# A hybrid decoder step: split MLP weights kept in DRAM, four MLP token groups, the RWKV solve on GpSimd, a planner with other latencies

## The chip, the cores and the metric

The kernel runs on 1 core of one Trainium2 chip. The time is the device time of one launch in microseconds (us), the median of the runs. Five engines work in parallel, each on its own in-order stream of instructions: PE (TensorE, matmuls), DVE (VectorE), ACT (ScalarE), POOL (GpSimd) and SP (SyncE, which here does nothing but issue DMAs). An instruction that waits for a semaphore holds back all that stands behind it on its engine.

## The reference

One decoder layer for 2048 prompt tokens and 64 sample tokens (8 sequences of 8), width 1024, all in f32:

```python
h = rms_norm(x, norm1_g) * (1.0 + sc1) + sh1
proj = h @ w_in                                   # 1024 -> 3328: q, k, v and the RWKV row P
att = combine_dilations(branches)                 # three dilated windows, 8 heads of 64
r, decay, kr, vr, kk, a, g = rwkv7_inputs(P, P_prev, ...)
o, S = wkv7_scan(wkv0, r, decay, kr, vr, kk, a)   # S = S*w + (S.-kk)(kk*a)' + v k', per token
mix = concat([att, rwkv7_output(o, ...)]) @ w_out
x = x + gt1 * mix
h2 = rms_norm(x, norm2_g) * (1.0 + sc2) + sh2
x = x + gt2 * (square(relu(h2 @ w_ff1)) @ w_ff2)  # 1024 -> 4096 -> 1024
y = rms_norm(x, normf_g)
```

The sample tokens attend to a cache of past keys and values and carry an RWKV state each.

## The kernel before

**Numbers.** Every large product is computed from f32 operands that are each split in two: `hi`, the value rounded to the matmul's fast f32 type, and `lo`, the rest. `mm3` makes three matmuls for each 128-row slice: hi by hi, hi by lo, lo by hi (L319, L320, L321). A weight block of 128x1024 numbers is therefore loaded (tile `stg`, 512 KB), copied to `hi` by ACT and subtracted to `lo`, five eighths of it by POOL and three eighths by DVE (`split`, L257 and L261). Tiles `whi`, `wlo` are blocks of w_in; `wh`, `wl` are blocks of w_out, w_ff1 and w_ff2 (`wload`).

**Stages.** The prompt goes in four windows of 512 tokens. `i0` to `i3` are the input projections, `a0` to `a3` the attention of a window (four head pairs each), `r0` to `r3` its RWKV part, `s` the sample tokens. RWKV works in groups of 128 tokens, four per window, 16 in all (and one for the sample). For each group `rw_elem` makes decays and vectors, `rw_mats` makes triangular matrices with PE (PSUM tile `aps`, result `AT`), `rw_solve` inverts them: two DMAs `dA<-AT` and `sol<-dA` spread 32 small 32x32 matrices over 128 partitions, 31 steps of two elementwise operations each run on `sol` (L707, L713, on DVE), DMAs `dT<-sol` and eight `AT<-dT` bring the result back, and PE finishes with two sets of small matmuls (`zps`, L725 and L729). `rw_chunk` then advances the state twice (`px`, `pu`, `psS`). The tile `sol` exists once; `AT`, `bkT` and `F1` exist once, so that the matrices of a group are made when the group before has been through `rw_chunk`.

**MLP.** Five token groups: three of 512, then 256 + 64 sample tokens, then 256. For group w, `m` loads the concatenated heads (`mixd`, in DRAM), `p` does w_out, residual and norm in halves of at most 320 tokens, `f` runs eight rounds of w_ff1 (four blocks) and w_ff2 (four blocks). Each group loads and splits every weight block again; w_out is loaded once per half. Group 3 needs the RWKV result of the first half of the last window, group 4 that of the second half. Group 4 has its own buffers, in memory that the vector stages have given up.

**Order.** A planner of the framework places the instructions of all engines by its own model of their durations, and by priorities that come from the string `ORDER`: `f2:8@2190-2740` says that eight rounds of group 2 belong to 2190 to 2740 of the plan's time. What the planner decides is the fixed order on each engine. MLP and input matmuls (PSUM tile `mmps`) are what PE does while the vector stages run.

Of the kernel before, what the change touches and what calls it, by code (L numbers as in the profile page):

```python
# [18 lines left out]
D = 1024  # L19
KD = 8  # L20
# [20 lines left out]
m3@2730-2731 f2:99@2740-2741 p3@2741-2790 f3:2@2790-2990 m4@2840-2841 p4@2841-2890 f3:99@2840-3040  # L41
f4:99@3000-3200
# [79 lines left out]
class Step:  # L122
    def __init__(self, tc, I, O):
        self.tc, self.nc, self.I, self.O = tc, tc.nc, I, O
        self.es = ExitStack()
        self.bg = None
        self.lo_eng, self.nw, self.nwb = [tc.nc.gpsimd], 0, 0
# [14 lines left out]
    def setup(self):  # L142
# [18 lines left out]
        self.mixd = self.dr.tile([D, SEQ + NS], F32, name="mixd")  # L161

# [92 lines left out]
    def split(self, hi, lo, src, eng=None):  # L255
# [17 lines left out]
    def norm_B(self, xt, pool, rows, A, B, hhi, hlo, c0, sample, psp, pstag):  # L273
        nc = self.nc
        h32 = pool.tile([128, KD, 128], F32, name="h32", tag="h32")
        for hb in range(2):
# [29 lines left out]
            eng = nc.vector if hb else nc.gpsimd  # L306
            eng.tensor_tensor(lo, h32[:, sl, 0:rows], hi.bitcast(F32), op=ALU.subtract)  # L307
# [23 lines left out]
    def w_in(self, c0, G):  # L331
        nc = self.nc
# [4 lines left out]
        for h in range(2):  # L337
            sl = slice(128 * h, 128 * h + 128)
            sg = G.tile([128, KD, 128], F32, name="stg", tag="stg")
            src = self.I["w_in"][0][:, c0 + 128 * h:c0 + 128 * h + 128]  # L340
            nc.sync.dma_start(sg, src.rearrange("(k p) c -> p k c", p=128))
            self.split(hi[:, :, sl], lo[:, :, sl], sg)
# [116 lines left out]
    def rwkv_setup(self):  # L459
# [8 lines left out]
        self.masks_s = cst("masks_s", [128, 128])  # L468
# [161 lines left out]
    def rw_mats(self, V, psv, r, nch, masks):  # L630
# [8 lines left out]
        AO = V.tile([64, nch * 8, 64], F32, name="AO", tag="AO")  # L639
# [7 lines left out]
        for c in range(nch):  # L647
# [6 lines left out]
            for par in (1, 0):  # L654
# [10 lines left out]
        r.update(F1=F1, bkT=bkT, AT=AT, AO=AO)  # L665
# [3 lines left out]
    def rw_bonus(self, V, psv, r):  # L669
# [12 lines left out]
    def rw_solve(self, V, psv, r, nch):  # L682
# [6 lines left out]
        for b in range(2):  # L689
            o = 32 * b  # L690
            nc.sync.dma_start(dA[:, b].rearrange("u s t -> s u t"), AT[o:o + 32, :, o:o + 32])
# [12 lines left out]
        for s in range(31):  # L704
            m, n = 31 - s, s // 4 + 1
            t3 = tmp[:, 0:m * n].rearrange("p (j i) -> p j i", i=m)
            nc.vector.tensor_tensor(  # L707
# [5 lines left out]
            nc.vector.tensor_tensor(T[:, 0:n, s + 1:32], T[:, 0:n, s + 1:32], t3, op=ALU.add)  # L713
# [5 lines left out]
        nc.vector.transpose(TZ[0:32, 0], AT[64:96, :, 0:32])  # L719
# [4 lines left out]
        for u in range(nu):  # L724
            nc.tensor.matmul(pz[96:128, u], AT[0:32, u, 32:64], TZ[0:32, 0, u], start=True, stop=True, tile_position=(0, 96))  # L725
# [6 lines left out]
    def rw_chunk(self, V, psv, r, c, nxt, po):  # L732
# [23 lines left out]
        nc.gpsimd.tensor_tensor(s0, UV[0:64, c], dcb, op=ALU.mult)  # L756
# [73 lines left out]
    def rwkv_window(self, w, V, psv):  # L830
# [8 lines left out]
        for g in range(g0, g0 + 4):  # L839
# [5 lines left out]
            for par in range(2):  # L845
                for c in range(2):
                    for o in (0, 64) if par else (0,):
                        nc.gpsimd.tensor_copy(
# [41 lines left out]
    def att_window(self, w, hp, V, psv):  # L890
# [10 lines left out]
        if w > 0:  # L901
            nc.gpsimd.dma_start(kT[:, :, :, 0:w], self.kTd[hp][:, :, :, 0:w])
# [145 lines left out]
    def rwkv_sample(self, V, psv):  # L1048
# [36 lines left out]
        self.rw_mats(V, psv, r, 1, self.masks_s)  # L1085
# [195 lines left out]
    def wload(self, src, n, G):  # L1281

        nc = self.nc
        nk = 1024 // n
        sg = G.tile([128, nk, n], F32, name="stg", tag="stg")
        nc.sync.dma_start(sg, src.rearrange("(k p) c -> p k c", p=128))
        hi = G.tile([128, nk, n], F32R, name="wh", tag="wh")
        lo = G.tile([128, nk, n], F32R, name="wl", tag="wl")
        self.nw += 1
        self.split(hi, lo, sg, self.lo_eng[self.nw % len(self.lo_eng)])  # L1290
# [343 lines left out]
```

## Time and profile before

| | |
|---|---|
| Time, median of 3 runs | 3894.37 us (3886.09 to 3895.49) |
| The profiled execution | 3875.28 us, its span 3873.5 us |
| PE busy | 3376.6 us (87%) |
| DVE, ACT, POOL busy | 2425.2 (63%), 1690.4 (44%), 1052.3 us (27%) |
| DMA | 505.27 MB, 43.3% of the 16 engines' time on SP's queue |
| Granted PE clock | 0.935 of full speed, mean |

Full speed of PE is 2.4 GHz; the lower of its two levels is 1.2 GHz, and a mean of 0.94 in a stretch says how long it was at either. PE idle is the length of a stretch less PE busy. A matmul's own duration in a row is longer than the distance to the next one, since matmuls overlap; the pace is read from a stretch without idle time. In the rows by windows the five busy times are, in this order, those of PE, PEld (weight loads), DVE, ACT and POOL, with the count of instructions behind each.

### The profile page before, as it was taken

The page shows a single profiled execution, that of the slowest core. Times are in us where ns is not written, and L with a number is a line of the kernel's source. Part 1 is how long each engine was busy: PE and PEld are TensorE (multiplying, and loading weights), DVE is VectorE, ACT ScalarE, POOL GpSimd, SP SyncE. Part 2 cuts the span into 40 slices and gives each one's busy share as a digit, 9 for nine tenths or more (in the row PEclk, how much of TensorE's full clock was granted, in tenths as well). Part 3 has the DMA queues.
Part 4 walks back from the last instruction along what each step waited for, and adds up shares of the span by engine and source line. Part 5 has one row for each costly group of instructions (what it writes and reads, how often), then busy time and mean ns, then how long its engine had stood idle before and what let it go on. Part 6 is the DMA issues. An engine that isn't in the chain of part 4 may idle for free. (4 is left out here: it accounts for less than half of the span.)

```text
span 3873.5 us, 64002 instructions
## 1 busy us (share of the span) xinstructions
PE 3376.6 (87%) x24050; PEld 2838.8 (73%) x24050; DVE 2425.2 (63%) x6052; ACT 1690.4 (44%) x3088; POOL 1052.3 (27%) x792
## 2 busy tenths in 40 slices
PE   7998898887978888898889898888889898869998
PEld 5875787777767666777767676676667776769998
DVE  3653665654656577877656765454777777645666
ACT  4542443453344355545434532344545344434354
POOL 2322231221133211223321121132112222234464
PEclk9999999888889999999999999999999999879999
DMA  7346644344243342325435244886432234354464
GB/s 245 112 138 184 169 124 129 109 84 93 78 116 119 100 129 76 100 85 168 124 98 142 75 91 118 244 256 202 124 104 85 86 88 135 110 148 142 144 188 153
DMA packets 698128, 505.27 MB, mean 130 GB/s; under 512 B 90330, under 2 KB 646540, under 8 KB 697820
## 3 DMA queue, kind: packets, MB, share of 16 engines
q1 hardware_dynamic: 685196, 488.54, 43.3%
q0 software_dynamic: 12624, 12.65, 1.3%
q8 instruction: 190, 3.11, 0.3%
q14 instruction: 118, 0.97, 0.1%
HBM read 430.77 MB, written 65.99 MB: 128 GB/s over the span
## 5 line engine op out<-in xcount | busy, mean ns | idle before, releaser
L261 POOL TENSOR_TENSOR wl<-stg,wh 128x640 fp32r<-128x640 f32 (+1 forms) x384 | 670.5, 1747 | 1655.9 <-ACT wh L257 1392.6
L257 ACT ACTIVATE wh<-stg 128x1024 fp32r<-128x1024 f32 x384 | 406.0, 1058 | 730.0 <-PE mmps L320 444.5
L319 PE MATMUL mmps<-h2hi,wh 128*128 128x256 f32 (+2 forms) x1864 | 635.8, 342 | 34.6 <-ACT wh L257 16.6
L321 PE MATMUL mmps<-h2hi,wl 128*128 128x256 f32 (+2 forms) x1864 | 635.8, 341 | 8.1 <-POOL wl L261 7.5
L320 PE MATMUL mmps<-h2lo,wh 128*128 128x256 f32 (+2 forms) x1864 | 632.7, 340 | 4.4 <-POOL h2lo L307 4.4
L320 PE MATMUL mmps<-hid,wh 128*128 128x512 f32 (+2 forms) x1280 | 469.9, 367 | 10.9 <-DVE hid L1388 10.8
L261 DVE TENSOR_TENSOR wl<-stg,wh 128x384 fp32r<-128x384 f32 (+1 forms) x384 | 304.2, 793 | 273.9 <-ACT wh L257 263.5
L319 PE MATMUL mmps<-hid,wh 128*128 128x512 f32 (+2 forms) x1280 | 469.9, 368 | 3.9 <-ACT acc L1274 2.8
L321 PE MATMUL mmps<-hid,wl 128*128 128x512 f32 (+2 forms) x1280 | 468.9, 367 | 1.1 <-POOL wl L261 0.9
L319 PEld LDWEIGHTS mmps<-h2hi,wh 128*128 128x128 f32 x1864 | 366.0, 197 | 68.7 <-ACT wh L257 18.0
L321 PEld LDWEIGHTS mmps<-h2hi,wl 128*128 128x128 f32 x1864 | 366.2, 196 | 40.0 <-POOL wl L261 9.4
L320 PEld LDWEIGHTS mmps<-h2lo,wh 128*128 128x128 f32 x1864 | 365.8, 196 | 34.5 <-POOL h2lo L307 5.1
L261 POOL TENSOR_TENSOR wlo<-stg,whi 128x640 fp32r<-128x640 f32 x104 | 183.8, 1781 | 588.2 <-ACT whi L257 523.0
L320 PEld LDWEIGHTS mmps<-hid,wh 128*128 128x128 f32 x1280 | 249.0, 195 | 45.0 <-DVE hid L1388 14.0
L319 PEld LDWEIGHTS mmps<-hid,wh 128*128 128x128 f32 x1280 | 248.3, 194 | 36.6 <-ACT acc L1274 3.4
L321 PEld LDWEIGHTS mmps<-hid,wl 128*128 128x128 f32 x1280 | 248.9, 194 | 32.0 <-issue 1.3
L1266 DVE SCALAR_TENSOR_TENSOR acc<-mmps,ada,acc 128x512 f32<-128x512 f32 (+1 forms) x280 | 179.0, 641 | 142.1 <-PE mmps L321 140.2
L319 PE MATMUL mmps<-whi,hhi 128*128 128x256 f32 (+1 forms) x816 | 242.8, 298 | 5.7 <-ACT qev L427 5.7
L320 PE MATMUL mmps<-wlo,hhi 128*128 128x256 f32 (+1 forms) x816 | 243.4, 298 | 1.2 <-POOL wlo L261 1.2
L319 PE MATMUL mmps<-hhi,whi 128*128 128x512 f32 (+2 forms) x608 | 223.5, 369 | 23.5 <-ACT pev L397 18.1
L321 PE MATMUL mmps<-whi,hlo 128*128 128x256 f32 (+1 forms) x816 | 242.7, 297 | 0.0
L320 PE MATMUL mmps<-hlo,whi 128*128 128x512 f32 (+2 forms) x608 | 222.3, 366 | 5.3 <-POOL hlo L307 5.3
(340 smaller groups left out, 6705.5 us busy)
## 6 DMA issues: line engine op xcount, KB each, us to landing
stg<-in_w_ff_dram SPq DMA_DIRECT2D x320, 512.0 KB
stg<-in_w_in_dram SPq DMA_DIRECT2D x104, 512.0 KB
stg<-in_w_out_dram SPq DMA_DIRECT2D x64, 512.0 KB
kst<-in_cache_k_dram SPq DMA_DIRECT2D x80, 256.0 KB
vst<-in_cache_v_dram SPq DMA_DIRECT2D x80, 256.0 KB
xt<-in_x_prompt_dram SPq DMA_DIRECT2D x32, 512.0 KB
wada<-in_w_ada_dram SPq DMA_DIRECT2D x32, 512.0 KB
Pd<-pev SPq DMA_DIRECT2D x56, 256.0 KB
```

What stands on the lines that cost most here:

```text
L257: nc.scalar.activation(hi, src, AF.Copy)
L261: eng.tensor_tensor(lo[:, k], src[:, k], hi[:, k].bitcast(F32), op=ALU.subtract)
L319: nc.tensor.matmul(out, wh(k), xh(k), start=k == 0, stop=False)
L320: nc.tensor.matmul(out, wh(k), xl(k), start=False, stop=False)
L321: nc.tensor.matmul(out, wl(k), xh(k), start=False, stop=k == nk - 1)
L1266: nc.vector.scalar_tensor_tensor(o, pt[:, 0:np_], gt[:, ob, 0:1], o, op0=ALU.mult, op1=ALU.add)
```

## The change

1. `wload` and `w_in` go through a new `weights`. After a given use of a block (the first for w_out and w_ff1, the second for w_ff2, the ninth for w_in, which has four) its `hi` and `lo` are written to DRAM; later uses load both, 512 KB each, with four DMAs, and split nothing. `stg`, `wh` and `wl` share seven buffers (three, three and two before).
2. Groups 3 and 4 become one of 512 + 64 tokens, in columns of 288. It takes its activations in the memory of the vector stages and its other buffers from the earlier groups.
3. The 31 steps of `rw_solve` run on POOL. `AT`, `bkT`, `F1` have two buffers, `AO` moves into `AT`; other small operations go from POOL to DVE; 32 loads of w_ada go to POOL's queue, 12 loads of `kT` to SP's.
4. `PlanCosts` changes the planner's model: 105 cycles more for each access, 2300 ns for a DMA's start, 0.443 ns for a PE cycle.

```diff
-m3@2730-2731 f2:99@2740-2741 p3@2741-2790 f3:2@2790-2990 m4@2840-2841 p4@2841-2890 f3:99@2840-3040
-f4:99@3000-3200
+m3@2730-2731 f2:99@2740-2741 p3@2741-2790 f3:99@2790-3200
...
+        self.done, self.uses, self.keep_at = set(), {}, {"in": 9, "out": 1, "ff1": 1, "ff2": 2}
...
-        self.nc.sync.dma_start(w, src.rearrange("(k p) c -> p k c", p=128))
+        (self.nc.sync if nk > 1 else self.nc.gpsimd).dma_start(w, src.rearrange("(k p) c -> p k c", p=128))
...
+    def weights(self, name, i, src, hi, lo, G, tag):
+
+        nc = self.nc
+        wd = self.wd[name][i]
+        if (name, i) in self.done:
+            for j, t in enumerate((hi, lo)):
+                for p in (slice(0, 64), slice(64, 128)):
+                    nc.sync.dma_start(t[p].bitcast(F32).rearrange("p k c -> p (k c)"), wd[p, j])
+            return
+        nk, n = lo.shape[1:3]
+        m = 1024 // nk
+        for c in range(0, n, m):
+            sg = G.tile([128, nk, m], F32, name="stg", tag=tag)
+            nc.sync.dma_start(sg, src[:, c:c + m].rearrange("(k p) c -> p k c", p=128))
+            self.split(hi[:, :, c:c + m], lo[:, :, c:c + m], sg)
+        self.uses[name, i] = n = self.uses.get((name, i), 0) + 1
+        if n == self.keep_at[name]:
+            for j, t in enumerate((hi, lo)):
+                nc.sync.dma_start(wd[:, j], t.bitcast(F32).rearrange("p k c -> p (k c)"))
+            self.done.add((name, i))
...
-                nc.vector.tensor_tensor(AT[0:64, u:u + 4], pt[0:64, :, 0:64], mb(0, 0, 64), op=ALU.mult)
-                nc.vector.tensor_tensor(AO[:, u:u + 4], pt[0:64, :, 64:128], mb(0, 64, 64), op=ALU.mult)
+                nc.vector.tensor_tensor(AT[64:128, u:u + 4], pt[0:64, :, 0:64], mb(0, 0, 64), op=ALU.mult)
+                nc.vector.tensor_tensor(AT[0:64, u:u + 4], pt[0:64, :, 64:128], mb(0, 64, 64), op=ALU.mult)
...
-            nc.vector.tensor_tensor(
+            nc.gpsimd.tensor_tensor(
                 t3,
                 A[:, s:s + 1, s + 1:32].to_broadcast([128, n, m]),
                 T[:, 0:n, s:s + 1].to_broadcast([128, n, m]),
                 op=ALU.mult,
             )
-            nc.vector.tensor_tensor(T[:, 0:n, s + 1:32], T[:, 0:n, s + 1:32], t3, op=ALU.add)
+            nc.gpsimd.tensor_tensor(T[:, 0:n, s + 1:32], T[:, 0:n, s + 1:32], t3, op=ALU.add)
...
-        raw=2, rawl=1, e2=8, F=2, bk=1, F1=1, bkT=1, AT=1, AO=1, UV=2, xx=2, Dt=1, lm=2, sgl=2, bv=1, xs=1,
+        raw=2, rawl=1, e2=7, F=2, bk=1, F1=2, bkT=2, AT=2, UV=2, xx=2, Dt=1, lm=2, sgl=2, bv=1, xs=1,
...
-    gs = [pt(512 * w, 4) for w in range(3)] + [pt(1536, 2) + [(SEQ, NS, True)], pt(1792, 2)]
-    MG = dict(h2h=1, h2l=1, acc=1, wh=3, wl=3, stg=2, hid=NHID, st=4, rlu=2)
+    gs = [pt(512 * w, 4) for w in range(3)] + [pt(1536, 4) + [(SEQ, NS, True)]]
+    MG = dict(h2h=1, h2l=1, acc=1, w=7, hid=NHID, st=4, rlu=2)
...
-                X = Tags(gm.enter_context(right("last")), {**MG, "hid": 5, "stg": 3, "wh": 4, "wl": 4, "rlu": 2})
...
+                X = Tags(gm.enter_context(right("last")), dict(h2h=1, h2l=1, acc=1))
+                B = S.mlp_tiles(TS + NS, X)
+                G = Mix(G, h2h=X, h2l=X, acc=X)
...
+    ACCESS, DMA, CYCLE = 105, 2300.0, 0.443
...
+        for k in T.ACCESS_CYCLES:
+            T.ACCESS_CYCLES[k] += self.ACCESS
+        T.DMA_START_FIXED_NS, T.PE_CYCLE = self.DMA, self.CYCLE
...
-    with tile.TileContext(nc) as tc:
+    with PlanCosts(), tile.TileContext(nc) as tc:
```

The planner's order changes everywhere. Three places are shown: the order of one engine before and after.

PE, before, where the last group of the last window waits for its solve: `aps` are its matrices, `zps` uses the solved ones, `mmps` of 320 columns are MLP matmuls of group 3.

```order
L321 MATMUL mmps<-h2hi,wl 128x320
L319 MATMUL mmps<-h2hi,wh 128x320
L320 MATMUL mmps<-h2lo,wh 128x320
L658 MATMUL aps<-F,bk 128x128 x8
...
L321 MATMUL mmps<-hid,wl 128x320
L319 MATMUL mmps<-hid,wh 128x320
L320 MATMUL mmps<-hid,wh 128x320
L725 MATMUL zps<-sol,AT 32x32 x16
```

PE, after, at the same place, up to where the MLP of the last token group begins:

```order
L674 MATMUL aps<-F,bk 128x128 x3
L785 MATMUL psS<-UV,bkT 64x64 x8
L839 MATMUL gps<-sgl,r_g_1770 128x128 x4
...
L741 MATMUL zps<-sol,AT 32x32 x16
L745 MATMUL zps<-AT,sol 32x32 x16
...
L885 MATMUL stps<-ident,state 128x64 x4
...
L343 MATMUL mmps<-h2hi,wh 128x256
```

Between the last `aps` and the first `zps` stood 302 MLP matmuls of 320 columns; now there is none, only RWKV matmuls of the group before. The same holds for the third group of the window (253 MLP matmuls before, none now).

POOL, before, in a stretch of the vector stages of the second half: parts of weight splits (`wl`), the clearing of `sol`, and small RWKV operations.

```order
L261 TENSOR_TENSOR wl<-stg,wh 128x640 x3
L701 MEMSET sol 128x256
L703 MEMSET sol 32x8 x4
L261 TENSOR_TENSOR wl<-stg,wh 128x640
L261 TENSOR_TENSOR wl<-stg,wh 128x512 x2
L848 COPY DC<-Dt 64x4 x6
L756 TENSOR_TENSOR xs<-UV,DC 64x512
```

POOL, after, at the end of one solve and the start of the next, in the third window:

```order
L723 TENSOR_TENSOR sol<-sol 128x28
L729 TENSOR_TENSOR sol<-sol 128x7x4
L265 TENSOR_TENSOR wl<-stg,wh 128x512
L723 TENSOR_TENSOR sol<-sol 128x24
...
L265 TENSOR_TENSOR wl<-stg,wh 128x640
L717 MEMSET sol 128x256
L719 MEMSET sol 32x8 x4
L265 TENSOR_TENSOR wl<-stg,wh 128x640 x2
```

The 62 steps of a solve now stand on POOL as one block with at most four other instructions inside; weight splits of the first two token groups stand before and behind it.

SP, before, at the last solve of the last window: weight loads (`stg`) between the solve's DMAs.

```order
L691 DMA dA<-AT 32x16x32 x2
L1286 DMA stg<-in_w_ff_dram 128x4x256
L502 DMA raw<-Pd 128x4x129
L698 DMA sol<-dA 128x1x1024
L1286 DMA stg<-in_w_ff_dram 128x4x256 x3
```

SP, after, at the first solve of the same window: each block now comes as two halves of `wh` and two of `wl`.

```order
L707 DMA dA<-AT 32x16x32 x2
L519 DMA raw<-Pd 128x4x129 x2
L714 DMA sol<-dA 128x1x1024
L274 DMA wl<-wd_ff_122 64x1024 x2
L274 DMA wh<-wd_ff_151 64x1024 x2
L730 DMA dT<-sol 128x256
```

Where one DMA carried a block, four do, and they stand between the steps of the solve.

## Rows read from the trace of the kernel before

**Rows 1.** The page: its head, and the busy time of each engine.

```profile
span 3873.5 us, 64002 instructions
...
PE 3376.6 (87%) x24050; PEld 2838.8 (73%) x24050; DVE 2425.2 (63%) x6052; ACT 1690.4 (44%) x3088; POOL 1052.3 (27%) x792
```

**Rows 2.** Windows A to D: length, five engines' busy, PEclk, DMA share, GB/s.

```profile
0.00:138.00 138.00, 109.85 (x600) 84.20 (x601) 50.98 (x123) 65.66 (x117) 37.56 (x37) 0.95 0.64 211
138.00:2978.00 2840.00, 2474.84 (x17807) 2039.12 (x17805) 1804.16 (x4769) 1246.38 (x2345) 664.33 (x527) 0.94 0.45 126
2978.00:3440.00 462.00, 397.51 (x2708) 328.60 (x2708) 317.47 (x727) 191.67 (x346) 129.40 (x109) 0.91 0.36 105
3440.00:3873.50 433.50, 394.39 (x2938) 386.88 (x2937) 252.61 (x436) 186.67 (x280) 220.97 (x120) 0.96 0.52 160
```

**Rows 3.** Windows: 512-column MLP, 256-column MLP, sample attention, MLP alone.

```profile
1930.00:1960.00 30.00, 30.00 (x134) 24.86 (x133) 17.68 (x57) 11.49 (x15) 8.35 (x5) 1.00 0.28 73
3720.00:3790.00 70.00, 70.00 (x584) 69.88 (x583) 46.31 (x73) 34.18 (x49) 45.12 (x25) 1.00 0.60 182
...
2400.00:2700.00 300.00, 259.50 (x2309) 209.24 (x2308) 138.19 (x258) 115.66 (x196) 66.20 (x39) 0.95 0.77 231
...
3500.00:3700.00 200.00, 192.25 (x1340) 189.03 (x1341) 125.72 (x237) 86.02 (x131) 95.08 (x53) 1.00 0.47 145
```

**Rows 4.** Waits of PE: who waited for whom, total us, times, longest.

```profile
PE ptps L1019 <- ACT s L993: 40.1, 17, 3.3
PE zps L725 <- DVE sol L719: 37.3, 8, 7.8
...
PE s2ps L958 <- DVE kT L922: 26.0, 16, 3.5
PE trps L1436 <- DVE xt L1439: 19.2, 12, 6.4
PE btps L645 <- DVE bk L620: 18.5, 5, 7.0
PE mmps L319 <- ACT pev L397: 18.1, 7, 4.9
PE mmps L319 <- ACT wh L257: 16.6, 3, 12.2
...
PE trps L1436 <- ACT acc L1268: 15.1, 14, 2.6
```

**Rows 5.** Groups of instructions: busy us, mean ns of one, idle before them.

```profile
L261 DVE TENSOR_TENSOR wl<-stg,wh 128x384 fp32r<-128x384 f32 (+1 forms) x384 | 304.2, 793 | 273.9 <-ACT wh L257 263.5 <-PE mmps L321 4.7 <-ACT st L1423 1.7
...
L713 DVE TENSOR_TENSOR sol<-sol 128x60 f32<-128x60 f32 (+24 forms) x527 | 144.6, 274 | 11.2
```

**Rows 6.** POOL: copies `DC` (min/median/max ns), and one subtraction in two sizes.

```profile
L848 POOL COPY DC<-Dt x96: 181/347/4742, 136.5 to 3218.8; 64x4 f32<-64x4 f32 x96
...
L526 POOL TENSOR_TENSOR bnl<-mr,bnh 128x512 fp32r<-128x512 f32 x16 | 21.3, 1332 | 83.1 <-ACT bnh L525 83.1
...
L526 POOL TENSOR_TENSOR bnl<-mr,bnh 128x256 fp32r<-128x256 f32 x1 | 0.7, 724 | 3.7 <-ACT bnh L525 3.7
```

**Rows 7.** Timeline, one group of r3, then the last's end: start, us, instruction.

```profile
2988.45 1.71 PE L658 MATMUL aps<-F,bk 64*128 64x128 f32 x16
...
3005.42 0.19 DVE L707 TENSOR_TENSOR sol<-sol 128x31 f32<-128x31 f32 x1 [4.95 <-DMA sol<-dA]
...
3040.85 0.34 SPq L714 DMA_DIRECT2D dT<-sol  x1
...
3051.41 1.19 PE L725 MATMUL zps<-sol,AT 32*32 32x32 f32 x32
...
3421.09 1.17 PE L729 MATMUL zps<-AT,sol 32*32 32x32 f32 x32 [0.30 <-issue]
...
3457.73 0.58 PE L319 MATMUL mmps<-h2hi,wh 128*128 128x256 f32 x1 [12.20 <-ACT wh L257]
```

**Rows 8.** Waits of SP's queue: the longest in total.

```profile
SPq L1286 <- DVE wl L261: 1249.0, 346, 14.7
```

More of the change, by code (lines that the diff above doesn't have):

```diff
@@ L161, in setup @@
         self.mixd = self.dr.tile([D, SEQ + NS], F32, name="mixd")
+        self.wd = {
+            name: [self.dr.tile([128, 2, m], F32, name=f"wd_{name}{i}") for i in range(n)]
+            for name, n, m in (("in", 13, 2048), ("out", 8, 1024), ("ff1", 32, 1024), ("ff2", 32, 1024))
+        }
+        self.done, self.uses, self.keep_at = set(), {}, {"in": 9, "out": 1, "ff1": 1, "ff2": 2}
     def params(self, G, psp):
@@ L253, in mod, with split @@
         return A, self.ada[:, 8 * sh:8 * sh + 8]
-    def split(self, hi, lo, src, eng=None):
+    def split(self, hi, lo, src):
         nc = self.nc
@@ L336, in w_in @@
         hi = G.tile([128, KD, 256], F32R, name="whi", tag=tag)
[L337 to L342, printed above, removed]
+        self.weights("in", c0 // 256, self.I["w_in"][0][:, c0:c0 + 256], hi, lo, G, "stg")
         return hi, lo
@@ L724, in rw_solve @@
         for u in range(nu):
-            nc.tensor.matmul(pz[96:128, u], AT[0:32, u, 32:64], TZ[0:32, 0, u], start=True, stop=True, tile_position=(0, 96))
+            nc.tensor.matmul(pz[96:128, u], AT[64:96, u, 32:64], TZ[64:96, 0, u], start=True, stop=True, tile_position=(64, 96))
         nc.scalar.activation(TZ[96:128, 0], pz[96:128], AF.Copy)
@@ L1084, in rwkv_sample @@
         r = self.rw_elem(V, psv, -1)
-        self.rw_mats(V, psv, r, 1, self.masks_s)
+        masks = V.tile([128, 128], F32, name="masks_s", tag="masks_s")
+        nc.sync.dma_start(masks, I["masks_s"])
+        self.rw_mats(V, psv, r, 1, masks)
         self.rw_solve(V, psv, r, 1)
@@ L1279, in gate_s, with wload @@
             self.nc.vector.tensor_tensor(a[:, k], a[:, k], gt[:, k, 1:9, None].to_broadcast([128, 8, 8]), op=ALU.mult)
-    def wload(self, src, n, G):
-        nc = self.nc
+    def wload(self, name, i, src, n, G):
         nk = 1024 // n
[L1285 to L1290, printed above, removed]
+        hi = G.tile([128, nk, n], F32R, name="wh", tag="w")
+        lo = G.tile([128, nk, n], F32R, name="wl", tag="w")
+        self.weights(name, i, src, hi, lo, G, "w")
         return hi, lo
@@ L1314, in mlp_mix @@
             for k in range(0, KD, nk):
-                sg = G.tile([128, nk, n], F32, name="stg", tag="stg")
+                sg = G.tile([128, nk, n], F32, name="stg", tag="w")
                 nc.sync.dma_start(
@@ L1333, in mlp_prep @@
             for ob in range(KD):
-                hi, lo = self.wload(I["w_out"][0][:, 128 * ob:128 * ob + 128], 128, G)
+                hi, lo = self.wload("out", ob, I["w_out"][0][:, 128 * ob:128 * ob + 128], 128, G)
                 pt = psg.tile([128, 512], F32, name="mmps", tag="mm")
@@ L1371, in ff1 @@
             for fb in fbs:
-                hi, lo = self.wload(I["w_ff1"][0][:, 128 * fb:128 * fb + 128], 128, G)
-                hd = G.tile([128, 2, T], F32R, name="hid", tag="hid")
+                hi, lo = self.wload("ff1", fb, I["w_ff1"][0][:, 128 * fb:128 * fb + 128], 128, G)
+                hd = G.tile([128, 2, TS + NS], F32R, name="hid", tag="hid")
                 W.append((hi, lo, hd))
@@ L1413, in mlp_ff @@
         c = 0
-        gf = G.tile([128, D], F32, name="gf", tag="wl")
+        gf = G.tile([128, D], F32, name="gf", tag="w")
         nc.sync.dma_start(gf, I["normf_g"].rearrange("(o d) -> o d", o=1).to_broadcast([128, D]))
@@ L1573, in tile_hybrid_step, with __enter__, __exit__ @@
     S.es.close()
+class PlanCosts:
+    ACCESS, DMA, CYCLE = 105, 2300.0, 0.443
+    def __enter__(self):
+        from concourse.hw_specs import TRN2Spec as T
+        self.T, self.old = T, (dict(T.ACCESS_CYCLES), T.DMA_START_FIXED_NS, T.PE_CYCLE)
+        for k in T.ACCESS_CYCLES:
+            T.ACCESS_CYCLES[k] += self.ACCESS
+        T.DMA_START_FIXED_NS, T.PE_CYCLE = self.DMA, self.CYCLE
+    def __exit__(self, *_):
+        T = self.T
+        T.ACCESS_CYCLES.update(self.old[0])
+        T.DMA_START_FIXED_NS, T.PE_CYCLE = self.old[1:]
 class Mix:
     def __init__(self, base, **other):
-        self.base, self.other = base, other
+        self.base, self.other, self.b = base, other, base.b
     def tile(self, shape, dt, name, tag, bufs=None):
```

33 lines of the change are left out of this document (12 added, 21 removed).

## The prediction

> **What bounds the kernel now.** I read four views in this order: the page, the table by windows, the waits, and a timeline of one RWKV group. The page shows PE busy for 87% of the span and no other engine over 63% [rows 1]. PE is the bound, and a gain can only come from what PE loses. The table by windows splits the loss. Stretch A is the start, B everything up to the last window's RWKV part, C that part, D the rest [rows 2]. In each, the length less PE busy is idle time: A 28, B 365, C 64.5, D 39, together 497 us. The length times (1 − PEclk) is what the clock takes: 7, 170, 42, 17, together 236. What is left is 3873.5 − 497 − 236 = 3140 us of matmuls at full speed. So B holds 535 of 733 lost us, and its DVE is busy 1804 of 2840 us, more than any engine but PE with its loads.
>
> That the granted clock follows idle time is seen in rows: with PE never idle it is 1.00, and over 300 us of sample attention with 40 us idle it is 0.95, a mix of 2.4 and 1.2 GHz [rows 3]. In B the clock takes 170/365 = 0.47 us for each idle us. I use that ratio below.
>
> The waits say for whom PE stands still [rows 4]: no single pair is large. ACT's softmax (`ptps`) costs 40.1, the solve (`zps`) 37.3, five pairs of small DVE and ACT results (26.0, 19.2, 18.5, 18.1, 15.1) 96.9, split weights (`wh`) 16.6. The rest of B's 365 is spread thin.
>
> **The change, part by part.**
>
> *PE work.* The number of matmuls and their columns stay; 1464 matmuls of 256 columns and 1464 of 320 become 2928 of 288. PE takes 30 us/134 = 224 ns for 512 columns and 70/584 = 120 ns for 256 [rows 3]. On the line through both, 288 columns take 133 ns and 320 take 146, so the exchange costs nothing. The 3140 us stay.
>
> *Splits removed.* Of 384 block splits 104 stay and 280 go; 216 blocks come back from DRAM in both halves, 72 are written once. DVE loses 280 × 793 ns = 222 us [rows 5]. PE waited only 16.6 us for weights [rows 4], and I take 12 of these as saved. The direct gain is small; the indirect one is DVE's freed time, below.
>
> *DMAs.* SP issues 728 more loads and stores at 0.34 us [rows 7], 248 us. It now waits 1249 us for `wl` splits [rows 8], and that covers them; if the cover is gone, the solve's own DMAs, which stand on the same queue, come later. The bytes grow by 216 + 72 − 280 × 0.5 = 148 MB. Sample attention already moves 231 GB/s at a DMA share of 0.77 [rows 3]. I take 0 and keep up to 40 us for the range. The 32 loads of w_ada go to POOL, which is busy 38 of the first 138 us [rows 2], and the 12 of `kT` cost SP 4 us: 0 for both.
>
> *Solve on POOL, price.* No two-operand step of this size runs on POOL before. A step is 50 columns on average. POOL's subtraction gains 1332 − 724 = 608 ns over 256 columns, 2.375 ns each, so 50 cost 119 ns [rows 6]. The fixed part lies between 724 − 608 = 116 ns and the copies `DC`, whose minimum is 181 and median 347 ns. That gives 0.235, 0.300 or 0.466 us for each of 62 steps, or 14.6, 18.6 or 28.9 us for a solve. I take 18.6, since the copy is the nearest row in size and its minimum is the operation without a neighbour. On DVE the steps average 274 ns, 17 us pure, but the solve in the timeline lasts from 3005.42 to 3040.85, 35 us, because other DVE work stands between them [rows 5, 7]. On POOL almost nothing stands between. What comes behind a solve on POOL now waits for all of it: five eighths of a split in the first two MLP groups, for which PE waits in the end. A block is 24 matmuls, 5.4 us at 512 columns, and three blocks lie ahead, 16 us; against 18.6 that is 2.6 us for each of eight solves, 21 at most. The solve seldom meets the end of that cover: 0, and 21 for the range.
>
> *The chain of a group.* From the last `aps` (2990.16) to the first step 15.2 us; the solve; from `dT` (3040.85) to `zps` 10.6 us [rows 7]; I estimate 4 more to the second `zps`. With 18.6 this is 48.4, say 49 us.
>
> *Stretch C.* PE's order after the change has no MLP matmuls between `aps` and `zps` in the last two groups, and few in the first two: 180 of 512 columns, 41 us, where 798 of 512 and 600 of 320 (269 us) stood. Group 3 of the MLP now begins only after the last solve. So C becomes the bare chain: 4 × 49, 3 × 10 between groups, 6 for the last state, and 37 from the last `zps` (3421.09) to the first MLP matmul (3457.73) [rows 7], 269 us. PE has about 100 us of RWKV and MLP work inside; 170 are idle, and I add 35 for the clock: 205 where 64.5 + 42 = 106 were lost. **This part costs 99 us.** Stretch D gives 12 us of the start of the MLP to C and may gain or lose a little by one group in place of two: 50 for 56. A stays at 35.
>
> *Stretch B.* Here is what should pay.
>  - `ptps`: more MLP matmuls now stand between scores and transposed probabilities, 4.1 to 9 us in place of 1.7 to 5.2 (counted in PE's order, at the pace of rows 3, as the covers below). The mean wait is 40.1/17 = 2.4 us, the longest 3.3 [rows 4]: I take 33 of 40.1.
>  - The five pairs of DVE and ACT results: DVE loses 13 solves of 62 × 274 ns (221 us) and some 170 splits (135 us), and gets some 65 us of POOL's small operations. Its busy time in B falls from 1804 to 1513 us, from 63.5% to 53%. Waiting behind other work goes as u/(1 − u), 1.74 to 1.13, minus 35%; the solves are also the longest blocks in front of a small result. I take two thirds, 65 of 96.9; ends one third and all.
>  - Weights 12, as above, and a tenth (17 us) of the idle time with no name.
>  - `zps`: the cover shrinks from 39–66 us of matmuls to 28–39, against 15.2 + 18.6 + 10.6 = 44 us of chain that other PE work covers in part; I add 23 us to 37.3.
>
>  Idle time in B: 365 − 33 − 65 − 12 − 17 + 23 = 261. Clock: 0.47 × 261 = 122. B loses 383 instead of 535, **a gain of 152 us.**
>
> *Sum.* 3140 + 35 + 383 + 205 + 50 = 3813 us of span. The profiled execution is 3875.28 with a span of 3873.5, 0.5% under the median of 3894.37. Against the median I add the same 21 us: **3834 us.** With one third or all of the five pairs, ±32 × 1.47 = ±47; with 14.6 us a solve, −4.0 × 16 × 1.4 = −90. So the forecast's own range is 3745 to 3880.
>
> **The rivals.** *Bigger gain.* With DVE relieved and the order laid by other latencies, B could run halfway to the MLP alone, where PE loses 3.9 us of 100 and the clock is 1.00 [rows 3]; over 2840 us that is 111. Halfway between 535 and 111 is about 320; with the zps cover holding too (−70) 250: a span of 3680, 3701 us. For it: no wait in B is large, all are short and of a kind that order can cover. Against: RWKV's chain is serial and its cover is shorter.
>
> *No change.* Two thirds of the relief: 127 × 2/3 = 85 − 23 = 62, idle 303, clock 142, 3875 of span, 3896 us.
>
> *Slower: the solve is dear on POOL.* If each step waits for its operands as the median `DC` copy does, a solve lasts 28.9 us, and 10.3 more stand in each of 16 chains that nothing covers: 165 us, and by the clock some 60 to 65: 4060 us. Halfway (0.383 us a step) it is 3950. From 0.35 us a step, C's loss and B's waits outweigh B's gain. For it: the same 64x4 copy takes 181 to 4742 ns [rows 6], so POOL is held up often. Against: much of what DVE did meanwhile is gone.
> The Trainium skill, "GPSIMD Engine Reference", section "Engine selection", sends elementwise work on a tile to VectorE and calls GpSimd about two times slower for two inputs. This speaks against the move; the trace bears it out in part, 1332 ns for 512 columns here against 793 for DVE's mostly 384 [rows 5, 6], a ratio by column of 1.26. By the page's factor a step would be an estimated 0.55 us, a solve 34 us, and the sum about 4170.
>
> *Slower: the relief was hidden anyway.* The splits went to engines with idle time, and SP's 1249 us of waiting [rows 8] shows weights ahead of need. If only `ptps` gains (33) and `zps` loses (23), B loses 355 + 167 = 522: 3973 us.
>
> **How the numbers follow.** Forecast 0.44, bigger gain 0.16, no change 0.10, dear solve 0.17, hidden relief 0.13. A measurement of this kernel can tell about 0.3%, 12 us, from no change: faster 0.44 + 0.16 = 0.60, same 0.10, slower 0.30. The range leaves out the dear half of the dear solve and a little beyond 3701 on the low side, with the 40 us of DMA: 3670 to 3990.
>
> **What would show it.** Right: POOL's solve steps near 0.30 us and a solve under 22 us; `zps` the largest wait of PE, most of it in C; C shortened to some 270 us and mostly idle; DVE busy near 53% in B, and the five pairs under 40 us together; `ptps` under 10; B's granted clock 0.95 to 0.96. Wrong: steps over 0.35 us or `zps` waits of 10 us and more in each group of B; SP behind on weights (PE waiting for DMAs `wh` or `wl`) in sample attention or in D; or C kept short because the chain is quicker than the rows say.

## The result, and the profile of the changed kernel

| | before | changed |
|---|---|---|
| Time, median | 3890.23 us (4 runs) | 4094.17 us (4 runs, 4091.06 to 4102.61) |
| Ratio | 1 | **1.0527**, 95% interval 1.0503 to 1.0551 |
| Profiled execution, span | 3873.5 us | 4089.3 us |
| PE busy / idle | 3376.6 / 496.9 us | 3416.2 / 673.1 us |

The changed kernel is 5.3% slower. The span is PE's busy time plus PE's idle time, and that ledger closes: 176 us more idle, 40 us more busy (the same 24050 matmuls, at a granted clock of 0.899 in place of 0.935), together 216.

The page of the changed kernel, its head and busy times [rows 1]:

```profile
span 4089.3 us, 63526 instructions
...
PE 3416.2 (84%) x24050; PEld 2874.9 (70%) x24050; DVE 1983.7 (49%) x4897; ACT 1420.7 (35%) x2808; POOL 755.3 (18%) x1407
```

Every engine but PE has less to do, DVE by 442 us. The relief that the prediction counted on is there, and yet the kernel is slower.

The windows, cut as in [rows 2]: start, all before the last window's RWKV part, that part, the rest.

```profile
0.00:138.00 138.00, 106.34 (x583) 81.63 (x583) 46.49 (x114) 60.71 (x106) 31.34 (x30) 0.91 0.64 207
138.00:3236.00 3098.00, 2633.79 (x18432) 2168.49 (x18431) 1614.98 (x4054) 1167.48 (x2278) 628.74 (x1109) 0.92 0.60 166
3236.00:3530.00 294.00, 182.41 (x1455) 141.37 (x1453) 144.99 (x315) 85.87 (x180) 87.88 (x263) 0.64 0.24 60
3530.00:4089.30 559.30, 493.62 (x3584) 483.41 (x3584) 177.20 (x416) 106.66 (x246) 7.30 (x5) 0.94 0.71 177
```

Length less PE busy gives PE's idle time: 32, 464, 112 and 66 us where it was 28, 365, 64.5 and 39. More than half of the added idle time (99 of 176 us) lies in B.

PE's waits (total us, times, longest), to be set against [rows 4]:

```profile
PE zps L741 <- DVE sol L735: 82.5, 8, 20.2
PE mmps L345 <- POOL wl L265: 51.6, 16, 14.3
PE mps L228 <- DMA wada<-in_w_ada_dram: 50.5, 16, 18.5
PE mmps L345 <- DMA wl<-wd_out: 50.0, 32, 13.6
PE s2ps L974 <- DVE kT L938: 32.7, 20, 4.7
PE trps L1449 <- DVE xt L1452: 31.5, 17, 5.6
...
PE trps L1449 <- ACT acc L1286: 19.3, 50, 0.6
...
PE mmps L344 <- POOL wlo L265: 17.1, 2, 16.8
PE btps L661 <- DVE bk L637: 14.6, 3, 11.9
...
PE mmps L343 <- ACT pev L415: 13.3, 5, 4.7
```

Weights now come late from POOL (`wl`, `wlo`, 69 us here; `wl` 8.3 us before), they come late from DRAM, which is new (`wd_out`, 50 us), and `zps` has doubled. The timeline of the first solve on POOL (start, us, instruction) shows what a solve is now:

```profile
188.72 0.24 POOL L723 TENSOR_TENSOR sol<-sol 128x31 f32<-128x31 f32 x1 [9.89 <-DMA sol<-dA]
189.03 1.33 POOL L729 TENSOR_TENSOR sol<-sol 128x31 f32<-128x31 f32 x1
190.44 0.27 POOL L723 TENSOR_TENSOR sol<-sol 128x30 f32<-128x30 f32 x1
190.79 0.28 POOL L729 TENSOR_TENSOR sol<-sol 128x30 f32<-128x30 f32 x1
...
213.91 0.21 POOL L729 TENSOR_TENSOR sol<-sol 128x8 f32<-128x8 f32 x1
214.07 3.02 POOL L265 TENSOR_TENSOR wlo<-stg,whi 128x640 fp32r<-128x640 f32 x2
```

A step of 0.27 us is followed by the next one after 0.35; some take 1.3. From 188.72 to 214.12 the solve lasts 25.4 us, and a weight split stands right behind it. Taken so from the first and last step of each, the 17 solves have a median of 26.8 us.

### The profile page after: what moved, and what is told of

Read it like the earlier page. It is cut to its first block, busy times and chain, and to the rows that moved or that the text cites. A ratio compares the mean times of both kernels' runs of the same rounds, so it can differ in the third digit from the quotient of the medians.

```text
span 4089.3 us, 63526 instructions
## 1 busy us (share of the span) xinstructions
PE 3416.2 (84%) x24050; PEld 2874.9 (70%) x24050; DVE 1983.7 (49%) x4897; ACT 1420.7 (35%) x2808; POOL 755.3 (18%) x1407
## 4 chain that ended last, share of the span: by engine, by line
PE 52%; DMA 19%; POOL 9%; DVE 7%; ACT 6%; issue 5%; SPq 2%; DVEq 0%; POOLq 0%; ACTq 0%
PE mmps L345 12%; PE mmps L343 12%; PE mmps L344 12%; POOL sol L723 4%; POOL sol L729 4%; DMA sol<-dA 3%; DMA wh<-wd_out 2%; DMA stg<-in_w_ff_dram 2%; PE pops L1025 2%; DMA xt<-in_x_prompt_dram 2%; DMA stg<-in_w_in_dram 2%; PE aps L674 2%; PE ptps L1035 2%; DMA kst<-in_cache_k_dram 1%; DVE ql L938 1%
## 5 line engine op out<-in xcount | busy, mean ns | idle before, releaser
L345 PE MATMUL mmps<-h2hi,wl 128*128 128x512 f32 (+3 forms) x1864 | 644.6, 346 | 71.1 <-DMA wl<-wd_out 50.0
L343 PE MATMUL mmps<-h2hi,wh 128*128 128x512 f32 (+3 forms) x1864 | 641.9, 344 | 44.5 <-DMA wh<-wd_out 26.3
L344 PE MATMUL mmps<-h2lo,wh 128*128 128x512 f32 (+3 forms) x1864 | 637.4, 342 | 0.7 <-DVE h2lo L331 0.7
L345 PE MATMUL mmps<-hid,wl 128*128 128x512 f32 (+1 forms) x1280 | 459.2, 360 | 33.7 <-POOL wl L265 32.8
L343 PE MATMUL mmps<-hid,wh 128*128 128x512 f32 (+1 forms) x1280 | 460.9, 360 | 7.7 <-DVE acc L1284 4.7
L344 PE MATMUL mmps<-hid,wh 128*128 128x512 f32 (+1 forms) x1280 | 460.1, 359 | 0.0
L265 POOL TENSOR_TENSOR wl<-stg,wh 128x512 fp32r<-128x512 f32 (+1 forms) x104 | 165.5, 1592 | 994.3 <-ACT wh L261 827.4
L1284 DVE SCALAR_TENSOR_TENSOR acc<-mmps,ada,acc 128x512 f32<-128x512 f32 (+2 forms) x280 | 179.7, 642 | 249.6 <-PE mmps L345 248.3
L1398 ACT ACTIVATE rlu<-mmps 128x512 f32<-128x512 f32 (+3 forms) x169 | 84.9, 504 | 596.9 <-PE mmps L345 589.6
L1400 DVE TENSOR_TENSOR rlu<-rlu 128x512 f32<-128x512 f32 (+3 forms) x169 | 99.7, 592 | 334.5 <-ACT hid L1399 334.0
L343 PE MATMUL mmps<-hhi,whi 128*128 128x512 f32 (+2 forms) x608 | 220.8, 365 | 22.1 <-ACT pev L415 13.3
L345 PE MATMUL mmps<-hhi,wlo 128*128 128x512 f32 (+2 forms) x608 | 217.2, 358 | 10.4 <-POOL wlo L265 10.4
```

Source lines behind the costliest of these rows:

```text
L343: nc.tensor.matmul(out, wh(k), xh(k), start=k == 0, stop=False)
L344: nc.tensor.matmul(out, wh(k), xl(k), start=False, stop=False)
L345: nc.tensor.matmul(out, wl(k), xh(k), start=False, stop=k == nk - 1)
L1284: nc.vector.scalar_tensor_tensor(o, pt[:, 0:np_], gt[:, ob, 0:1], o, op0=ALU.mult, op1=ALU.add)
L1398: nc.scalar.activation(rl[:, 0:n], pt[:, 0:n], AF.Relu)
L1400: nc.vector.tensor_tensor(rl[:, 0:n], rl[:, 0:n], rl[:, 0:n], op=ALU.mult)
```

## The experiments

Theories: 1, the solve on POOL is the loss; 2, the bytes of the kept weights; 3, the order (the planner's latencies, and four groups that leave the last window without cover); 4, added later, the shared buffers. All ratios are to the kernel before on the same chip.

### Chance of a placing

```diff
-    ACCESS, DMA, CYCLE = 105, 2300.0, 0.443
+    ACCESS, DMA, CYCLE = 100, 2300.0, 0.443
```

> The changed kernel with 100 instead of 105 cycles for each access in the planner's model, a change that should mean nothing but a new placing. It tells what a new placing alone is worth: I expect 4060 to 4130, and read no difference smaller than this run's from 4094 in the other runs.

4122.53 us, ratio 1.0637 [1.0565, 1.0708]. An edit without meaning moves the changed kernel by 1.1 points. This is a single pair, so the chance may be larger; differences of its size or less between two placings are not taken as effects of an edit below.

### Parts of the change undone, one at a time

The solve back on VectorE:

```diff
-            nc.gpsimd.tensor_tensor(
+            nc.vector.tensor_tensor(
                 t3,
...
-            nc.gpsimd.tensor_tensor(T[:, 0:n, s + 1:32], T[:, 0:n, s + 1:32], t3, op=ALU.add)
+            nc.vector.tensor_tensor(T[:, 0:n, s + 1:32], T[:, 0:n, s + 1:32], t3, op=ALU.add)
```

> The changed kernel with the 62 steps of each solve back on VectorE; all else as changed, the planner places anew. Theory 1 (the solve on GpSimd is the loss: it lasts some 26 us, and the weight splits behind it in the first two MLP groups make PE wait, 52 us for wl and 28 for wlo): the time falls by 80 to 130 us, to 3965 to 4015, and PE's waits for wl and wlo of GpSimd fall under 20 us together. Theory 2 (DMA traffic of the kept weights) and theory 3 (the order of the planner, and no MLP work as cover in the last window): within 40 us of 4094, or slower, since VectorE is loaded again.

3989.04 us, 1.0281 [1.0251, 1.0311]: 2.5 points, about 95 us of the kernel before on the same chip, come back. PE's wait for `wl` of POOL fell to 25.5 us, not under 20. But the solves themselves got longer, a median of 43.5 us from first to last step, since DVE does other work between. The length of a solve alone is not the loss.

The planner's own latencies again:

```diff
-    with PlanCosts(), tile.TileContext(nc) as tc:
+    with tile.TileContext(nc) as tc:
```

> The changed kernel without the planner's other latencies (PlanCosts). Theory 3 (the new order is the loss): the time falls by 80 us or more, to under 4015. Theories 1 and 2: it stays within 60 us of 4094, either way, and the order that hides shorter latencies makes the waits for zps longer than 82 us.

4276.46 us, 1.1022 [1.099, 1.1054]: further off than any theory gave. The new latencies are worth 5 points in the changed kernel. Theory 3 in this form falls.

No block of w_out, w_ff1 or w_ff2 kept:

```diff
-"out": 1, "ff1": 1, "ff2": 2}
+"out": 9, "ff1": 9, "ff2": 9}
```

> The changed kernel with no w_out, w_ff1, w_ff2 block kept in DRAM: every use splits again, as before the change. Theory 2 (loading both halves costs: PE waits 86 us for DMAs of wh and wl, DMA share 0.85 to 0.96 in sample attention): the time falls by 50 to 100 us, to 3995 to 4045. Theory 1: it rises, since more splits now stand on GpSimd behind the solves: 4150 or more, with PE's waits for wl of GpSimd over 100 us.

4084.69 us, 1.0527 [1.0458, 1.0597]: no difference. Late `wl` from POOL rose to 130.7 us, the late DMAs went away.

Five token groups again (the order string's last line and the groups as before; the last group's own weight buffers are eleven in one tag):

```diff
-    gs = [pt(512 * w, 4) for w in range(3)] + [pt(1536, 4) + [(SEQ, NS, True)]]
+    gs = [pt(512 * w, 4) for w in range(3)] + [pt(1536, 2) + [(SEQ, NS, True)], pt(1792, 2)]
```

> The changed kernel with the five MLP token groups of before (512, 512, 512, 256 + 64, 256), so that group 3 can again stand in front of the last two solves. Theory 3 in its second form (no cover in the last window: 112 us of PE idle and a clock of 0.64 there): the stretch of the last RWKV part is filled again and the time falls by 60 to 100 us, to 3995 to 4035. Theories 1 and 2: it falls by 30 us at most; a fifth group costs some 64 blocks of weights more to load, at 1 MB each.

4214.74 us, 1.0863 [1.0831, 1.0894]: slower, against the expectation. After the last solve the DMA share is 0.95 at 235 GB/s: a group of 256 tokens asks for as many bytes as one of 512 in half the time. How much of the loss is this, and how much the shared buffers (theory 4, below), the run does not separate.

The w_ada loads on SP:

```diff
-        (self.nc.sync if nk > 1 else self.nc.gpsimd).dma_start(w, src.rearrange("(k p) c -> p k c", p=128))
+        self.nc.sync.dma_start(w, src.rearrange("(k p) c -> p k c", p=128))
```

> The changed kernel with the 32 loads of w_ada back on SyncE's queue. If their place on GpSimd's queue, where they wait behind splits and solves, is what makes PE wait 50.5 us for them (36.8 before; the longest 18.5 us against 7.0), the time falls by 15 to 40 us, to 4055 to 4080, and PE is earlier by that much at 700 us already. If not: within 15 us of 4094.

4105.53 us, 1.0604 [1.0556, 1.0652]. PE still waits 48.4 us for them, so POOL's queue is not the reason. This wait goes with the place of the solve: it is 48 to 65 us in every run with the solve on POOL, on either queue, and 17 to 37 us in every run with the solve on DVE. Why is not shown.

### Parts done alone in the kernel before

The planner's latencies alone (the class `PlanCosts`, and one line):

```diff
-    with tile.TileContext(nc) as tc:
+    with PlanCosts(), tile.TileContext(nc) as tc:
```

> The kernel before with one edit: the planner's other latencies (PlanCosts). In the changed kernel their removal cost about 185 us, in an order string that was laid for them. If they are good by themselves, this kernel falls by 40 us or more, to under 3840; if they only belong to the changed order string, it stays within 40 us of the kernel before, or is slower.

3835.92 us, **0.9908** [0.9879, 0.9937]: 0.9% under the kernel before. With 100 cycles in place of 105:

> The kernel before with the planner's other latencies, with 100 cycles in place of 105 for each access. If the gain of 35 us is the latencies', it stays: under 3860. If it was one lucky placing: 3850 to 3900, about the kernel before.

3846.74 us, 0.9943 [0.9919, 0.9968]. Both placings are faster, but each by less than the 1.1 points that a placing alone was seen to move; that the latencies help by themselves is not shown. The solve on GpSimd alone, the first diff of this section's second part turned round:

> The kernel before with one edit: the 62 steps of each solve on GpSimd. Theory 1 (a solve lasts some 26 us there and blocks GpSimd's share of the weight splits, of which this kernel has four times as many): slower by 80 to 160 us, 3960 to 4040, with PE's waits for wl of GpSimd over 100 us in place of 8. My prediction's reasoning (VectorE freed by 220 us, a step 0.30 us): within 40 us of the kernel before or faster.

4064.06 us, 1.0497 [1.0467, 1.0528]. Slower by 193 us, more than the 80 to 160 of theory 1, with 113.9 us of PE waiting for `wl`. And with the latencies as well:

> The kernel before with the planner's other latencies and the solve on GpSimd. The solve alone cost 193 us there under the old latencies, the latencies alone gave 35. If the new latencies let the planner lay enough work over the solve, it is under 3900; if the cost is GpSimd's queue, which no order of PE takes away, it is 3950 to 4030.

3978.41 us, 1.0261 [1.02, 1.0323]: the second case, and 3.5 points above the same kernel with the solve on VectorE. Where these sit is shown by windows that run from the last `aps` of each group to its first `zps`, one for each of the 17 groups (PE first among the busy times). The first of the 17 and the sum, with the solve on VectorE and then on GpSimd:

```profile
164.30:271.90 107.60, 96.77 (x697) 86.93 (x697) 61.13 (x194) 43.97 (x81) 28.17 (x22) 0.90 0.50 143
...
sum 1318.40, PE 1098.20 PEld 944.94 DVE 915.25 ACT 550.33 POOL 392.31; mean PE 64.60 PEld 55.58 DVE 53.84 ACT 32.37 POOL 23.08
```

```profile
168.60:226.40 57.80, 40.15 (x328) 39.03 (x327) 28.83 (x99) 22.99 (x43) 30.12 (x74) 0.88 0.36 97
...
sum 1061.10, PE 737.71 PEld 633.34 DVE 469.57 ACT 365.07 POOL 548.09; mean PE 43.39 PEld 37.26 DVE 27.62 ACT 21.47 POOL 32.24
```

On VectorE the planner lays 64.6 us of PE work between `aps` and `zps`, and 1318 − 1098 = 220 us stay idle. On GpSimd it lays 43.4 us over a chain that takes 62.4 us (1061.1/17), and 323 us stay idle. These 103 us are most of the 120 us by which PE's idle time differs between the two kernels (3833.3 − 3341.1 = 492 and 3983.2 − 3371.3 = 612). The kernel before and its version with the solve on GpSimd read alike:

```profile
sum 1193.90, PE 1000.17 PEld 851.60 DVE 843.36 ACT 478.88 POOL 332.72; mean PE 58.83 PEld 50.09 DVE 49.61 ACT 28.17 POOL 19.57
```

```profile
sum 1065.40, PE 731.04 PEld 614.28 DVE 476.26 ACT 345.75 POOL 538.33; mean PE 43.00 PEld 36.13 DVE 28.02 ACT 20.34 POOL 31.67
```

194 us idle become 334. In the changed kernel the windows of two groups can overlap; the stretches that at least one of them covers hold 375 us of idle time (1179.0 − 803.9), and 277 us (1566.6 − 1289.4) with the solve back on VectorE. That is 98 of the 105 us by which PE's idle time differs between these two. So what the move of the solve costs is a cover that is laid too short for the chain.

The rival is that this cover itself waits for splits behind the solve. Booked by name, 163 of the 323 us are waits for splits on POOL, and 28 of the 220 with the solve on VectorE. In the rows of PE's waits over the whole kernel with the solve on GpSimd:

```profile
PE mmps L321 <- POOL wl L261: 133.7, 39, 23.2
...
PE zps L725 <- DVE sol L719: 51.5, 8, 22.3
```

With the solve on VectorE these two are 28.7 and 26.5 us. But with it on GpSimd the first `zps` starts, in ten of the 17 windows, within 0.1 us of the end of the last transpose of solved matrices (DVE, `sol<-AT`) that it needs, and over all 17 together 20 us after it. With the chain ending when it did, weights in time would have moved PE's waiting to `zps` and saved some 20 us at most.

Is it also the splits behind the solve on POOL?

```diff
-        m = n * 5 // 8
-        for eng, k in ((nc.gpsimd, slice(0, m)), (nc.vector, slice(m, n))):
+        for eng, k in ((nc.vector, slice(0, n)),):
```

> The changed kernel with every weight split's subtraction whole on VectorE, so that GpSimd does little but the solves. If the solve costs because GpSimd's share of the splits stands behind it (PE waited 52 us for wl and 28 us for wlo): 40 to 100 us less, 3995 to 4055, and VectorE busy some 250 us more. If it costs by its place in the chain of a group (waits for zps): within 25 us of 4094, zps waits as before.

4088.78 us, 1.0546 [1.0491, 1.0601]: nothing. The waits for POOL's splits are gone from the top of PE's waits, and others stand there:

```profile
PE zps L740 <- DVE sol L734: 90.6, 6, 16.0
PE mmps L342 <- ACT wh L261: 70.9, 13, 17.0
```

Taking away what waited behind the solve does not help while the chain itself outlasts the cover. One expectation failed: VectorE was busy 1976 us against 1984, not 250 more. 1024 columns of w_in take it 1226 ns; in the changed kernel its 384 of them take 800 ns and POOL's 640 take 1781. So POOL's share of this subtraction takes longer than the whole on VectorE alone. (Blocks of w_ff2 were shared half and half, not five to three.)

The weights kept, alone (the function `weights` for w_out and w_ff in the kernel before, with its own two `stg`, three `wh`, three `wl`):

> The kernel before with one edit: w_out, w_ff1 and w_ff2 blocks kept in DRAM after the same uses as in the changed kernel, each later load in four DMAs; the buffers stay three wh, three wl and two stg. Theory 2 (twice the bytes cost): slower by 30 to 100 us, with PE's waits for DMAs of wh and wl over 60 us, most of it in sample attention and at 256 columns. If removed splits are worth something: faster by 20 to 60 us.

4211.3 us, 1.0877 [1.0846, 1.0909], far beyond the expected loss. PE waits 111.8 us for `wl` of w_ff, and from the last solve to the end the DMA share is 0.94 at 234 GB/s:

```profile
3651.00:4213.70 562.70, 432.22 (x3093) 402.03 (x3090) 141.01 (x331) 76.74 (x172) 7.16 (x5) 0.94 0.94 234
```

Before, that stretch lasted 451.5 us.

### What is left with the solve on VectorE

> The changed kernel with the solve on VectorE and no w_out or w_ff block kept: four token groups, the planner's latencies, shared buffers and moved small steps are left. With the solve on GpSimd, keeping made no difference (4085 against 4094), but there the splits stood behind solves. If kept weights cost DMA time (58 us of PE's waits in the kernel with the solve on VectorE): 40 to 80 us under 3989, 3910 to 3950. If removed splits relieve VectorE by as much: within 30 us of 3989, either way.

4002.13 us, 1.0323 [1.0248, 1.0397]. And with five groups:

> The changed kernel with the solve on VectorE, nothing kept and five token groups: the planner's latencies, shared buffers, doubled matrices and moved small steps are left. If these small parts do nothing, it is the kernel before with the other latencies, 3836 (3825 to 3860). If four groups cost by the missing cover in the last window, it is 50 us or more faster than the run with four groups; if they save, slower.

4173.96 us, 1.0766 [1.0698, 1.0834], although it splits as the kernel before does. SP waits in it for PE's matmuls at the weight load, which it never did before [rows 8]. Theory 4 is that the seven shared buffers do this. Alone, in the kernel before with the planner's latencies:

```diff
-    MG = dict(h2h=1, h2l=1, acc=1, wh=3, wl=3, stg=2, hid=NHID, st=4, rlu=2)
+    MG = dict(h2h=1, h2l=1, acc=1, w=7, hid=NHID, st=4, rlu=2)
```

> The kernel before with the planner's other latencies, and stg, wh and wl in one tag of seven buffers (eleven in the last group) instead of 2 + 3 + 3 (3 + 4 + 4). Theory 4 (seven buffers in strict turn hold two and a third split blocks, so SyncE waits for PE's matmuls before it may load the next; in the five-group run these waits are 723 us and PE waits 280 us for wh and wl): slower than 3836 by 80 us or more, with SyncE waiting for PE at the weight load. If the buffers are innocent: within 25 us of 3836.

4215.2 us, 1.0876 [1.0796, 1.0955]: 9.7 points above the same kernel with separate buffers. The waits of SP's queue, then of PE:

```profile
SPq L1286 <- DVE wl L261: 564.0, 191, 14.9
SPq L1286 <- PE mmps L320: 454.3, 105, 14.9
SPq L1286 <- PE mmps L321: 382.7, 90, 10.8
```

```profile
PE mmps L319 <- ACT wh L257: 157.9, 99, 13.0
PE mmps L321 <- POOL wl L261: 127.0, 103, 2.4
```

A `stg` is free as soon as it is split, but in one tag it takes its turn behind `wh` and `wl`, which are free only when PE has used them. So SP waits 837 us for PE, and PE 285 us for weights. With separate buffers in the changed kernel (and `AT`, `bkT`, `F1` single, to make room):

> The changed kernel with the solve on VectorE, nothing kept, and separate buffers again (two stg, three wh, three wl; to make room AT, bkT and F1 single): four groups, the latencies and the small moved steps are left. Theory 4: 3840 to 3900, and PE's waits for wh and wl fall from 128 us to under 60. If four groups or the moved steps cost instead: within 30 us of 4002.

3970.28 us, 1.0244 [1.0175, 1.0312], 0.8 points under the shared buffers: with four groups they cost little, within the chance of a placing. Theory 4's 3840 to 3900 is missed; PE's waits for `wh` and `wl` fell from 128 to 85 us, not under 60. Kept weights with separate buffers:

> The same with the weights kept, as in the changed kernel. A kept block needs no stg, so of the eight buffers six are left, three blocks ahead. If keeping is worth nothing with enough buffers: within 30 us of the run without; if its DMAs cost as in the kernel before (340 us with five groups): slower by 60 us or more; if it relieves: faster by 20 to 60 us.

4039.62 us, 1.0423 [1.0348, 1.0497]: keeping costs 1.8 points here. And five groups once more, now with separate buffers:

> The changed kernel with the solve on VectorE, nothing kept, separate buffers and five token groups: of the change only the planner's latencies, the moved small steps and the moved loads are left. If four groups cost some 120 us, by leaving the last window's solves without MLP work and the last group whole behind them: 3820 to 3870, with 440 to 460 us after the last zps. If the moved steps are the rest: 3940 or more.

3899.46 us, 1.0079 [1.0056, 1.0103]. Four groups cost 1.65 points, some 64 us, not far above the chance of a placing. The windows from the last solve to the end, with four and with five groups:

```profile
3399.00:3968.30 569.30, 507.76 (x3739) 495.67 (x3737) 257.48 (x503) 186.68 (x326) 155.97 (x85) 0.92 0.31 93
```

```profile
3444.00:3892.60 448.60, 406.38 (x3093) 396.82 (x3090) 255.64 (x450) 191.81 (x288) 218.02 (x118) 0.94 0.51 155
```

With four groups PE has 101 us more work left when the solves end, which is the work that lay over the solves of the last window; the part before is only 45 us shorter.

What still separates this last kernel (1.0079) from the latencies alone (0.9908 and 0.9943) are the small steps moved from POOL to DVE, the moved loads and seven `e2` buffers: 1.4 to 1.7 points, not much over the chance of a placing. It was not split up further. From the latencies alone the whole change adds up as: small steps and loads 1.4 to 1.7 points, four groups 1.65, kept weights with shared buffers and doubled matrices 0.4 (1.0244 to 1.0281), the solve on POOL 2.5 (to 1.0527). Only the last is well above the chance of a placing.

## Why the prediction was wrong, step by step

**Forecast:** 3834 us and a range of 3670 to 3990; measured 4094. By the prediction's own ledger A and C came near (44 and 218 us lost, forecast 35 and 205) and D lost 99 for 50; what failed is the gain in stretch B, which lost 464 + 248 = 712 us where 383 were forecast, by the cover over the solve and the relief of DVE (below). The prediction's rival "the solve is dear on POOL" gave 4060. That this number is near is in part luck: the solve is about half of the loss (2.5 of 5.3 points), and it costs through the cover laid over it, since with it moved alone a whole solve is no longer on POOL than on DVE (medians 30.0 and 34.3 us).

- **Price of the solve: mis-sized.** I took 0.300 us a step and 18.6 us a solve. The steps' median duration was 292 ns, so the duration was right; but a step follows the last by 0.07 to 0.08 us more, and some take 1.3 us: 0.43 us from start to start in the mean. 26.8 us is near my upper bound of 28.9, which I had put aside. I added durations where a serial chain is paid in distances from start to start.
- **Chain of a group: too short.** 15.2 + 10.6 us around the solve came from one group of the last window. In the first group of the changed kernel it is 21.0 (last `aps` to 188.72) and 14.7 us (`dT` to `zps`). The whole chain is 61 us there, not 44.
- **Cover: the step that failed.** I compared it with 44 us and added 23 us to `zps` in B, for 60 in all. PE's wait that is booked on `zps` in B is 38.7 us, even less than that; but the loss is booked on other names, since what lies over the solve (splits, transposes) waits too. By the windows from `aps` to `zps` PE is idle for 103 and 140 us more in the two kernels where only the solve moved, and for 98 us more in the changed kernel than with its solve back on DVE.
- **Relief of DVE: the other step that failed.** Its busy share in B fell to 1615/3098 = 52%, as forecast (53%). `ptps` waits fell to 10.4 us (5.3 and 5.1), as forecast (7). The five pairs of DVE and ACT results should have fallen from 97 to 32 us; they are 32.7 + 31.5 + 14.6 + 13.3 + 19.3 = 111. My rule u/(1 − u) for waiting behind other work did not hold for them. That they are links of chains, which an engine's load does not shorten, is my reading; no run tests it.
- **Weights: wrong sign.** I saved 12 us of 16.6. PE now waits 69 us for splits on POOL and 76 us for loads of w_out (50.0 `wl`, 26.3 `wh`). The sum for splits behind a solve (at most 21) counted three blocks ahead, which the seven shared buffers do not hold: at three a block they hold two and a third.
- **Kept weights:** 0, with 40 us for the range. In the changed kernel it is 0; in three other arrangements it ran from −0.4 to +8.8 points. The largest, with five groups, also differs in the planner's latencies; that four groups are what makes keeping bearable fits the saturated DMA there (share 0.94), but was not tested alone.
- **Stretch C: right in kind.** Forecast 269 us long with 170 idle; measured 294 with 112 idle, at a clock of 0.64. D lost 27 us of idle time more, where I had forecast a small gain.
- **Planner's latencies: no term.** They are worth 5 points in the changed kernel. Alone in the kernel before they give 0.6 to 0.9%, which is within the chance of a placing.
- **The ledger itself was not closed.** I took 3140 us as work free of both losses. The same formula on the changed kernel gives 4089.3 − 673 − 400 = 3016 us for the same matmuls, because a stretch that is idle at a low clock is counted twice. Stretch C of the changed kernel shows it: (1 − 0.64) × 294 = 106 us are booked on the clock there, but its 182 us of busy time can lose half at most, 91, even if all of it ran at the lower of the two levels. PE busy and PE idle add up to the span; the clock belongs to the busy time alone.

The Trainium skill's "GPSIMD Engine Reference", section "Engine selection", puts elementwise work with two inputs at about twice VectorE's time on GpSimd. Here the medians are 292 and 211 ns for the same step (L723 in the changed kernel, L707 before), a factor of 1.4. The move lost time, as the page's advice has it, but not by the page's factor: a whole solve was no longer on POOL. On wide operations the page's factor holds: the weight split's 512 columns take 1662 ns on POOL and 829 on DVE in the kernel before, a factor of 2.0. The prediction's ratio of 1.26 by column is misread: its 793 ns are a mean over 224 operations of 384 columns and 160 of 512, and its 1332 ns belong to another operation.

What stays open: why the planner lays a shorter cover over a solve on POOL (its own duration for these steps was not read), whether the planner's latencies help by themselves, and how the last 1.4 to 1.7 points are shared out.

## What to carry to other kernels

A serial chain of small operations is paid by the distance from start to start, and what it costs is its length less the work that the order lays over it: measure PE's idle time between the chain's two ends, whatever name each wait carries. Before several edits are joined, try each alone: here the one that changes only the planner's numbers does not lose (0.6 to 0.9% faster, within the chance of a placing), and three of the others lose 5 to 10% when added to the kernel before or to that one, while they partly hide each other in the joined one. Measure first how far an edit without meaning moves the time, and read nothing smaller as an effect. Buffers of different lifetimes in one rotating tag make the short-lived wait for the long-lived.

## What the runs showed that I had not expected

The engine that takes less time from first to last step of a solve gave the slower kernel: in the kernel before the median is 34.3 us on DVE and 30.0 on POOL, but the planner laid 58.8 us of PE work over the one and 43.0 over the other. A change of 5 cycles in the planner's model moved the changed kernel by 1.1 points, as much as several of the edits under study.
